# Ordering a decoder layer's instructions by a simulated timeline of all engines

## The chip, the cores and the metric

One core of one Trainium2 chip runs the whole program. The metric is device time in microseconds (us) of one execution, the median over several runs. Below, PE is the matmul engine, PEld its weight loads, DVE the vector engine, ACT the scalar engine, POOL the general engine (GpSimd) and SP the engine that issues most DMAs. A filler is a matmul that no step near it waits for.

## What is computed

One decoder layer over 1024 tokens of 1024 features, all in float32:

```python
x = LN(ALPHA * x + 0.5 * swiglu(x, ffn1))        # FFN1, 2816 hidden columns
z = x @ w_in                                     # 1024 x 3872
ret = retention(z[:, :2048])                     # 8 heads, chunks of 128 tokens
y   = rwkv7_scan(z[:, 2048:])                    # 8 heads of 64
    # per token: state = state*w - (state@kk) b^T + v k^T ;  y = state @ r
mixed = concat(silu(g) * groupnorm(ret), (groupnorm(y) + bonus) * gate)
x = LN(ALPHA * x + mixed @ w_out)
x = LN(ALPHA * x + 0.5 * swiglu(x, ffn2))        # FFN2
out = x + sigmoid(x @ w_gate + b) * (p @ w_proj) # PLE
```

## The kernel before

The three dense parts (FFN1, FFN2, PLE) run as blocked matmuls; float32 operands are split into a high and a low half, and `mm3` (L61 to L63) makes three matmuls of each pair. A part of FFN is written by `ffn_up` and `ffn_down`, which multiply seven products instead of eight per 2x2 block. Between FFN1 and FFN2 stands the `mixer`, in which this document is interested.

The mixer makes `z` in 28 column tiles (`z_tile`: two halves of 24 matmuls of 512 columns, weights from DMA and split by ACT and POOL); three more are made before it. A unit is a pair of RWKV heads over half of the tokens: eight units, named `u_h` for pair u and half h, in the order 0_0, 0_1, 1_0, ... 3_1. Each goes through these steps, all of small matmuls (64 to 256 columns) with DVE and ACT work between them:

1. `rw_inputs` and `rw_operands` read z, form the unit's operands, and write the strictly triangular matrices M (`m1pw`, copied at L1003);
2. `substitution` inverts the diagonal 32x32 blocks of eight such matrices: M goes out to DRAM and back as `iltw`, 31 pairs of tiny DVE operations follow (`itw` L1033 and `ixw` L1035, each needing the one before), the result goes out and comes back as `Xd`;
3. `doublings` builds the full inverse from it: a DVE transpose (`XTw`, L1047), then matmuls i1 to i5 with DVE operations between;
4. `rw_chunks` goes through four chunks of tokens one after the other; each needs the state `wst` that the one before left (L1095, L1131, L1135), makes `scpw` and `chw` on PE and masked copies `scz` (L1107, L1108) on DVE;
5. a group norm (`gstw`, `gnyw`, L797 to L805), four PE transposes `ytpw` (L812), the gate, and a DMA into `mixed`.

`retention` does the like for the retention heads (names ending in r; `yor`, `gnyr`, `ytpr`). `w_out_group` reads `mixed` back, splits it (`mw`), multiplies (`wopo`, 96 matmuls per group of two operands, 384 in all) and adds into `xacc` (L1192). Substitution of unit n+1 is written so that it can run beside the chunks of unit n.

The program states each step once. A scheduler decides where it stands on its engine: it keeps an engine's queue in the order of priorities, and code can push a step back by a number. The z tiles that unit 0_0 does not need and nearly all `wopo` are pushed back by 300:

```python
FILLER = -300
fill = {-1: ("w1", "t0"), 0: ("w2",), 1: ("t1",), 2: ("w3",), 3: ("t2",), 4: ("t3",)}
rows = {5: [((4, 0), (0, 1))], 6: [((5, 1), (0, 1))], 7: [((6, 2), (0, 1)), ((7, 3), (0,))]}
...
with self.tc.issue_after(self.gate):
    for f in fill.get(s, ()):
        with self.tc.high_priority(offset=FILLER):
            (rw if f[0] == "w" else rt)(int(f[1]))
```

`self.gate` is an instruction of the last `m1pw` (L1001). The fillers of unit s may not be placed ahead of it. After the last unit `normalise` begins layer norm LN2 and `w_out_group((7, 3), ..., (1,), True)` makes the last half group; FFN2's weights (`f2w`) are loaded from L101.

## Time and profile before

| what | value |
|---|---|
| median of 3 runs | 2365.26 us (2356.21 to 2366.05) |
| profiled execution | 2365.46 us, span of the trace 2363.3 us |
| PE busy | 96% of the span |
| PEld busy | 77% |
| DVE, ACT, POOL busy | 69%, 36%, 32% |
| mean granted TensorE clock | 0.977 of full speed |

The span is the time from the first to the last record. The 2.2 us around it belong to the execution and stand in every time. A busy share is an average over stages that have different limits, so the shares of single stages are needed as well.

### The profile page before, as it was taken

To read this page: it belongs to the slowest core of one execution; us is meant where nothing else is said; L and a number is where in the kernel's file an instruction comes from. 1 tells how busy PE (TensorE), PEld (TensorE's weight loads), DVE (VectorE), ACT (ScalarE), POOL (GpSimd) and SP (SyncE) were. 2 spreads that over 40 slices of the span, in tenths; PEclk is the share of its full clock that TensorE was granted. 3 is DMA by queue.
4 is the path that set the end of the run, shared out by engine and by line. 5 is a ranking of instruction groups with operands and counts; after the bars stand their busy time and mean duration, and the time that the engine had idled before them with its cause. 6 is when DMAs were issued, how large, how long until landed. Compare 5 with 4: busy or idle time off the path is not lost.

```text
span 2363.3 us, 30893 instructions
## 1 busy us (share of the span) xinstructions
PE 2262.3 (96%) x10753; PEld 1818.2 (77%) x10753; DVE 1622.9 (69%) x2702; ACT 842.7 (36%) x1430; POOL 751.9 (32%) x614
## 2 busy tenths in 40 slices
PE   6999999999999899999899999988999999999999
PEld 5788888788786677777677777766888788788787
DVE  7677777665782487773864876679676767866862
ACT  4323232344643433322322322264323232445550
POOL 3336454300102323332432423225555453000220
PEclk9999999999999999999999999999999999999999
DMA  4345555497336343323333353322465544974321
GB/s 144 112 155 181 182 179 165 149 337 239 90 133 199 116 124 99 108 79 93 113 92 112 98 175 120 98 89 85 156 196 161 188 159 139 350 257 155 112 76 41
DMA packets 288945, 345.97 MB, mean 146 GB/s; under 512 B 35571, under 2 KB 162134, under 8 KB 288790
## 3 DMA queue, kind: packets, MB, share of 16 engines
q1 hardware_dynamic: 284208, 331.37, 43.6%
q0 software_dynamic: 3328, 12.06, 1.3%
q8 instruction: 85, 1.39, 0.2%
q10 hardware_dynamic: 1254, 0.58, 0.1%
q14 instruction: 70, 0.57, 0.1%
HBM read 237.50 MB, written 106.43 MB: 146 GB/s over the span
## 4 chain that ended last, share of the span: by engine, by line
PE 79%; DVE 14%; issue 2%; ACT 2%; DMA 1%; POOL 1%; SPq 0%; DVEq 0%; ACTq 0%; POOLq 0%
PE f1m L61 6%; PE f1m L62 6%; PE f1m L63 6%; PE f2m L61 5%; PE f2m L63 5%; PE f2m L62 5%; PE z L63 3%; PE z L61 3%; PE z L62 3%; DVE ixw L1035 2%; DVE itw L1033 2%; PE f1qa L62 1%; PE f1qa L61 1%; PE scpw L1099 1%; PE f1qa L63 1%
## 5 line engine op out<-in xcount | busy, mean ns | idle before, releaser
L63 PE MATMUL z<-x1Th,lo_win 128*128 128x512 f32 x448 | 191.3, 427 | 5.3 <-DVE lo_win L48 2.9
L61 PE MATMUL z<-x1Th,hi_win 128*128 128x512 f32 x448 | 191.1, 427 | 0.8 <-ACT hi_win L47 0.8
L62 PE MATMUL z<-x1Tl,hi_win 128*128 128x512 f32 x448 | 187.9, 420 | 0.0
L48 POOL TENSOR_TENSOR lo_win<-raw_win,hi_win 128x512 fp32r<-128x512 f32 x54 | 74.7, 1384 | 160.3 <-ACT hi_win L47 140.3
L1033 DVE TENSOR_TENSOR itw<-iltw,ixw 32x31 f32<-32x31 f32 (+15 forms) x248 | 104.5, 421 | 29.8 <-DMA iltw<-scrw 14.3
L1035 DVE TENSOR_TENSOR ixw<-ixw,itw 32x31 f32<-32x31 f32 (+15 forms) x248 | 108.9, 439 | 4.0
L63 PEld LDWEIGHTS z<-x1Th,lo_win 128*128 128x128 f32 x448 | 87.2, 195 | 26.4 <-POOL lo_win L48 4.0
L61 PEld LDWEIGHTS z<-x1Th,hi_win 128*128 128x128 f32 x448 | 87.5, 195 | 24.2 <-issue 3.8
L62 PEld LDWEIGHTS z<-x1Tl,hi_win 128*128 128x128 f32 x448 | 87.5, 195 | 20.3 <-issue 2.9
L149 POOL TENSOR_TENSOR f2tb<-f2tb,f2tb 128x512 f32<-128x512 f32 x44 | 71.9, 1634 | 91.5 <-DMA f2tb<-in_ffn_w_down 83.6
L48 DVE TENSOR_TENSOR f1hl<-f1s,f1hh 128x512 fp32r<-128x512 f32 x63 | 45.5, 723 | 61.6 <-ACT f1hh L47 61.6
L149 POOL TENSOR_TENSOR f1tb<-f1tb,f1tb 128x512 f32<-128x512 f32 x44 | 66.5, 1511 | 42.2 <-DMA f1tb<-in_ffn_w_down 35.7
L48 DVE TENSOR_TENSOR f2hl<-f2s,f2hh 128x512 fp32r<-128x512 f32 x63 | 44.8, 711 | 44.9 <-ACT f2hh L47 44.9
L47 ACT CAST f1hh<-f1s 128x512 fp32r<-128x512 f32 x63 | 39.2, 622 | 92.1 <-PE f1qa L62 42.3
L47 ACT CAST f2hh<-f2s 128x512 fp32r<-128x512 f32 x63 | 39.2, 623 | 89.8 <-PE f2qa L62 36.1
L659 ACT COPY zs<-z 128x512 f32<-128x512 f32 x56 | 32.7, 583 | 97.2 <-PE z L63 84.9
L108 DVE TENSOR_TENSOR f2S<-f2w 128x512 f32<-128x512 f32 x22 | 17.5, 800 | 72.1 <-DMA f2w<-in_ffn_w_gu 67.3
L47 ACT CAST hi_win<-raw_win 128x512 fp32r<-128x512 f32 x56 | 34.6, 619 | 90.2 <-PE z L62 82.2
L48 POOL TENSOR_TENSOR f1A12l<-f1w,f1A12h 128x512 fp32r<-128x512 f32 x22 | 30.9, 1408 | 106.8 <-ACT f1A12h L47 106.8
L62 PE MATMUL f2qa<-f2vl,f2hh 128*128 128x512 f32 x164 | 63.9, 390 | 0.5 <-DVE f2vl L48 0.5
L62 PE MATMUL f1qa<-f1vl,f1hh 128*128 128x512 f32 x164 | 63.9, 389 | 0.0
L63 PE MATMUL f2qa<-f2vh,f2hl 128*128 128x512 f32 x164 | 63.8, 389 | 0.0
(785 smaller groups left out, 7197.9 us busy)
## 6 DMA issues: line engine op xcount, KB each, us to landing
f1w<-in_ffn_w_gu SPq DMA_DIRECT2D x44, 512.0 KB
f2w<-in_ffn_w_gu SPq DMA_DIRECT2D x44, 512.0 KB
f1s<-hd SPq DMA_DIRECT2D x63, 256.0 KB
f2s<-hd SPq DMA_DIRECT2D x63, 256.0 KB
zs<-zs SPq DMA_DIRECT2D x56, 256.0 KB
raw_win<-in_w_in SPq DMA_DIRECT2D x54, 256.0 KB
f1tb<-in_ffn_w_down SPq DMA_DIRECT2D x44, 256.0 KB
wt<-f1tb SPq DMA_DIRECT2D x44, 256.0 KB
```

Source lines behind the costliest of these rows:

```text
L47: self.last_split = self.nc.scalar.copy(hi, src).ins
L48: (eng or self.nc.vector).tensor_tensor(out=lo, in0=src, in1=hi, op=ALU.subtract)
L61: mm(ps, a[0], b[0], start=first, stop=False)
L62: mm(ps, a[0], b[1], start=False, stop=False)
L63: mm(ps, a[1], b[0], start=False, stop=last)
L108: sub = lambda o, a, b, op=ALU.subtract: V.tensor_tensor(out=o, in0=a, in1=b, op=op)
L149: nc.gpsimd.tensor_tensor(out=t, in0=a, in1=b, op=ALU.subtract)
L659: nc.scalar.copy(zs, ps)
L1033: nc.vector.tensor_tensor(out=t, in0=lt[:, j, j + 1:].unsqueeze(2).broadcast_to([B, n, c]), in1=x[:, j:j + 1, 0:c].broadcast_to([B, n, c]) ...
L1035: nc.vector.tensor_tensor(out=x[:, j + 1:, 0:c], in0=x[:, j + 1:, 0:c], in1=t, op=ALU.add)
L1099: nc.tensor.matmul(ps[e][:, 0:2 * P], kp[rr, cs], ar[rr, c].rearrange("p a t -> p (a t)"), start=True, stop=True)
```

## The change

```diff
@@ kernel()
-    with tile.TileContext(nc) as tc:
+    with tile.TileContext(nc, schedule_with_timeline_sim=True) as tc:
         hybrid_layer(tc, A)
```

The scheduler places the steps by a simulated timeline of all engines, where it used a plain estimate for each operation. Every instruction of the program stays, with its operands: 9615 on PE, 2704 on DVE, 1451 on ACT, 619 on POOL and 1177 on SP in either build. Only their order on each engine differs. The up products of FFN1 after the first block, the up products of FFN2 and nearly all of the down products keep their order on PE; the mixer is ordered anew. The number of fillers on PE in each stretch, counted in the two orders (a stretch begins with its unit's first i1):

| | ahead of 0_0 | 0_0 | 0_1 | 1_0 | 1_1 | 2_0 | 2_1 | 3_0 | 3_1 | behind |
|---|---|---|---|---|---|---|---|---|---|---|
| before | 432 | 59 | 157 | 104 | 220 | 111 | 225 | 63 | 63 | 294 |
| after | 398 | 226 | 192 | 144 | 192 | 192 | 96 | 192 | 48 | 48 |

**First place.** PE at the end of unit 1_0 (`chw1_03` is its last chunk, `ytpw1_0` waits for its group norm, `z640_..` are fillers, `i1w1_1..` begins the next unit). Before, 26 fillers stand between the last chunk and `ytpw1_0`, of which the first are:

```order
L1143 MATMUL chw1_03_9171<-saw1_03_9179,scz3_6355 128x64
L62 MATMUL z640_0_8662<-x1Tl5_3703,hi_win640_1_8658 128x512
L63 MATMUL z640_0_8662<-x1Th_3697,lo_win640_1_8659 128x512
L61 MATMUL z640_0_8662<-x1Th_3697,hi_win640_1_8658 128x512
L62 MATMUL z640_0_8662<-x1Tl6_3704,hi_win640_1_8658 128x512
...
L63 MATMUL z640_1_8690<-x1Th_3697,lo_win640_1_8659 128x512
L812 MATMUL ytpw1_0_9206<-ident_58,gnyw1_0_9196 128x128 x4
```

In the changed order, at the same place:

```order
L1142 MATMUL chw1_03_9171<-wvtw1_0_8155,scz3_6355 128x64
L1143 MATMUL chw1_03_9171<-saw1_03_9179,scz3_6355 128x64
L1113 MATMUL chw1_10_9837<-wst1_6361,arw1_1_8854 128x128
L812 MATMUL ytpw1_0_9206<-ident_58,gnyw1_0_9196 128x128 x4
L1056 MATMUL i1w1_10_9767<-Xd_6345,M11_6344 128x128 x4
L812 MATMUL ytpr1_0_9401<-ident_58,gnyr1_0_9386 128x128
L1000 MATMUL m1pw2_00_9619<-arw2_0_9614,bbw2_0_9616 128x128 x4
```

The fillers have moved away from this place: `ytpw` follows the last chunk with one matmul between them, and the next unit's i1 stands behind it. The ends of the other units read alike.

**Second place.** DVE at the group norm of unit 1_1 (`gstw1_1`, `gnyw1_1`), while the substitution of 2_0 (`itw2_0..`, `ixw2_0`) is under way in the order before:

```order
L797 TENSOR_REDUCE gstw1_1_9955<-yrw1_1_9824 128x8
L1033 TENSOR_TENSOR itw2_011_9674<-iltw2_0_9633,ixw2_0_9638 32x240
L798 TENSOR_SCALAR gstw1_1_9955<-gstw1_1_9955 128x8
L1035 TENSOR_TENSOR ixw2_0_9638<-ixw2_0_9638,itw2_011_9674 32x20x12
L799 TENSOR_TENSOR gnyw1_1_9956<-yrw1_1_9824,gstw1_1_9955 128x512
L1033 TENSOR_TENSOR itw2_012_9677<-iltw2_0_9633,ixw2_0_9638 32x247
L1035 TENSOR_TENSOR ixw2_0_9638<-ixw2_0_9638,itw2_012_9677 32x19x13
L968 TENSOR_SCALAR rnw2_1_10039<-rnw2_1_10039 128x8
```

In the changed order:

```order
L1047 STREAM_TRANSPOSE XTw2_0_10588<-Xd_6345 128x1024
L992 TENSOR_TENSOR arw2_1_10438<-kkw2_1_10050,ePw2_1_10020 128x4x128
L797 TENSOR_REDUCE gstw1_1_9955<-yrw1_1_9824 128x8
L797 TENSOR_REDUCE gstr1_1_10141<-yor1_1_10118 128x8
L754 SCALAR_TENSOR_TENSOR wrw3_0_10819<-wzrw3_0_10816,pcol_1830,smrw3_0_10820 128x512
L798 TENSOR_SCALAR gstw1_1_9955<-gstw1_1_9955 128x8
L798 TENSOR_SCALAR gstr1_1_10141<-gstr1_1_10141 128x8
L799 TENSOR_TENSOR gnyw1_1_9956<-yrw1_1_9824,gstw1_1_9955 128x512
```

The substitution has moved: all 62 operations for the next unit stand in the first chunk of a unit, and the other three chunks and the group norm are free of them. The group norms of both kinds of heads now alternate.

**Third place.** PE at the end of the last unit, 3_1 (`wopo5`, `wopo7_1` are the output products). Before:

```order
L872 MATMUL yor3_1_12908<-rst1_6358,zqr3_1_12857 128x128
L875 MATMUL yor3_1_12908<-vtr3_1_12879,rscr3_1_12893 128x64 x2
L63 MATMUL wopo5_0_0_1_12501<-mw_11826 128x512
L61 MATMUL wopo5_0_0_1_12501<-mw_11826 128x512
L62 MATMUL wopo5_0_0_1_12501<-mw_11826 128x512
L812 MATMUL ytpw3_1_12835<-ident_58,gnyw3_1_12825 128x128 x4
```

In the changed order:

```order
L1142 MATMUL chw3_13_12808<-wvtw3_1_12120,scz3_6355 128x64
L1143 MATMUL chw3_13_12808<-saw3_13_12816,scz3_6355 128x64
L812 MATMUL ytpw3_1_12835<-ident_58,gnyw3_1_12825 128x128 x4
L812 MATMUL ytpr3_1_12947<-ident_58,gnyr3_1_12932 128x128 x4
L61 MATMUL wopo7_1_0_0_13244<-mw_11826 128x512
L62 MATMUL wopo7_1_0_0_13244<-mw_11826 128x512
L61 MATMUL wopo7_1_1_0_13252<-mw_11826 128x512
```

Before, 294 fillers stand behind the last chunk of 3_1; in the changed order these are the 48 of `wopo7_1`, the last half group, which needs the group norm's result by way of `mixed`.

## Rows read from the trace of the kernel before

**Rows 1.** The page: busy time of the engines, and the chain that ended last.

```profile
PE 2262.3 (96%) x10753; PEld 1818.2 (77%) x10753; DVE 1622.9 (69%) x2702; ACT 842.7 (36%) x1430; POOL 751.9 (32%) x614
PE 79%; DVE 14%; issue 2%; ACT 2%; DMA 1%; POOL 1%; SPq 0%; DVEq 0%; ACTq 0%; POOLq 0%
```

**Rows 2.** Windows by stage: busy us and instructions per engine, granted clock, DMA.

```profile
core 0: us, PE busy (x) PEld busy (x) DVE busy (x) ACT busy (x) POOL busy (x), PEclk, DMA share, GB/s
300.00:400.00 100.00, 100.00 (x443) 82.81 (x442) 73.71 (x82) 28.37 (x44) 55.77 (x37) 1.00 0.53 171
718.00:870.00 152.00, 138.21 (x567) 99.25 (x567) 68.60 (x135) 57.69 (x93) 46.67 (x63) 0.97 0.47 144
1016.00:1198.00 182.00, 170.97 (x952) 133.43 (x951) 119.17 (x271) 54.53 (x106) 66.47 (x62) 0.95 0.32 97
1483.00:1560.00 77.00, 73.70 (x332) 57.32 (x331) 54.76 (x98) 24.41 (x37) 21.44 (x18) 0.98 0.30 97
1560.00:1660.00 100.00, 85.52 (x371) 67.30 (x370) 86.68 (x119) 54.75 (x91) 41.43 (x27) 0.91 0.32 101
```

**Rows 3.** The transposes that open the units' doublings: ns min/median/max, first and last start.

```profile
L1047 DVE STREAM_TRANSPOSE XTw<-Xd x8: 1226/1236/1245, 867.2 to 1436.2; 128x1024 f32<-128x1024 f32 x8
```

**Rows 4.** Windows of 10 us inside the mixer, same columns as Rows 2.

```profile
1140.00:1150.00 10.00, 6.04 (x31) 4.84 (x31) 9.97 (x16) 3.99 (x7) 8.08 (x7) 0.96 0.27 81
1160.00:1170.00 10.00, 8.68 (x40) 7.63 (x41) 8.68 (x21) 0.00 (x0) 2.67 (x3) 0.66 0.44 151
1290.00:1300.00 10.00, 10.00 (x53) 7.22 (x52) 1.40 (x5) 2.44 (x6) 0.89 (x2) 1.00 0.18 45
```

**Rows 5.** Groups by line, whole trace and two tiles: busy, mean; or ns min/median/max.

```profile
L1033 DVE TENSOR_TENSOR itw<-iltw,ixw 32x31 f32<-32x31 f32 (+15 forms) x248 | 104.5, 421 | 29.8 <-DMA iltw<-scrw 14.3
L1035 DVE TENSOR_TENSOR ixw<-ixw,itw 32x31 f32<-32x31 f32 (+15 forms) x248 | 108.9, 439 | 4.0
L992 DVE TENSOR_TENSOR arw<-kkw,ePw x8: 671/691/1773, 779.2 to 1334.5; 128x512 f32<-128x512 f32 x8
```

**Rows 6.** Timeline at the end of unit 2_0: start, us, engine, operation.

```profile
1236.21 0.27 ACT L1144 COPY yrw<-chw 128x128 f32<-128x128 f32 x1 [1.34 <-PE chw L1143]
1237.80 0.67 DVE L797 TENSOR_REDUCE gstw<-yrw 128x8 f32<-128x512 f32 x1
1242.64 0.68 DVE L805 TENSOR_TENSOR gnyw<-gnyw,gstw 128x512 f32<-128x512 f32 x1
1243.38 0.65 PE L812 MATMUL ytpw<-ident,gnyw 128*128 128x128 f32 x4
1243.79 0.48 PE L63 MATMUL z<-x1Th,lo_win 128*128 128x512 f32 x1
```

**Rows 7.** Timeline of DVE around the substitution of unit 3_1.

```profile
1363.51 0.74 DVE L1003 COPY_PREDICATED M<-mask,m1pw 128x512 f32<-128x512 uint8 x1 [0.95 <-PE m1pw L1000]
1371.37 0.18 DVE L1033 TENSOR_TENSOR itw<-iltw,ixw 32x31 f32<-32x31 f32 x1 [4.89 <-DMA iltw<-scrw]
1418.41 0.17 DVE L1035 TENSOR_TENSOR ixw<-ixw,itw 32x31 f32<-32x31 f32 x1
1436.24 1.24 DVE L1047 STREAM_TRANSPOSE XTw<-Xd 128x1024 f32<-128x1024 f32 x1
```

**Rows 8.** Timeline behind the last chunk of unit 3_1.

```profile
1481.20 0.27 ACT L1144 COPY yrw<-chw 128x128 f32<-128x128 f32 x1 [2.12 <-PE chw L1143]
1492.12 0.60 PE L812 MATMUL ytpw<-ident,gnyw 128*128 128x128 f32 x4
1496.63 0.32 SPq L1155 DMA_DIRECT2D mixed<-wow  x1
1528.53 0.33 SPq L1169 DMA_DIRECT2D wo<-mixed  x1
1528.91 30.52 SPq L101 DMA_DIRECT2D f2w<-in_ffn_w_gu  x4
```

## The prediction

> **What bounds the kernel now.** I read the page first. PE is busy 96% of the span and makes up 79% of the chain that ended last, with DVE second at 14% [rows 1]. Where PE waits, the reader must look by stage. The windows show two kinds of stage [rows 2]. In FFN1 (300 to 400 us) PE runs 443 matmuls in 100 us, one each 0.226 us, with its weight loads busy 82.81 of 100 and the clock at 1.00: nothing is to be had there by order. In the mixer the weight loads are busy 99.25 of 152 us (65%), then 133.43 of 182 (73%): PE has room. The mixer runs from about 718 to 1560 us, 842 us, and it is the only long stage whose order changes.
>
> What the mixer holds of PE work I price from these rows. A filler costs 0.226 us as in FFN1. Units 1_0 and 1_1 (1016 to 1198 us) hold 952 matmuls, of which 104 + 220 = 324 are fillers by the count in the order, 73 us. The other 628 are small: four transposes of 128 columns take 0.41 us until the next matmul starts [rows 6], 0.10 each, and with 0.01 to 0.02 more for changes between large and small I take 0.115, so 72 us, or 36 us for each unit. That is 145 of 182 us. The other 37 us, some 18 a unit, are waits and slow stretches. What they wait for the 10 us windows show [rows 4]: at 1140 DVE is busy 9.97 and PE 6.04, and shortly after the clock is at 0.66 of full speed, between its 1.2 and 2.4 GHz levels within the window; at 1290 DVE is busy 1.40 and PE 10.00. Work for the two engines comes in turns.
>
> **The change part by part.** No instruction is added or removed, so the sum is one of waits. I use three marks that the transposes of Xd give [rows 3]. The first unit's is at 867.2 us, the last unit's at 1436.2, so before it is 149 us from 718 to the first, 569 for seven units (81.3 each), and 124 from the last to 1560.
>
> *Ahead of the first unit.* 398 fillers for 432: 34 x 0.226 = 8 us less, so 141. The rest of this stretch waits for the inputs of unit 0_0 either way.
>
> *Units 0_0 to 2_0.* They now hold 226 + 192 + 144 + 192 + 192 = 946 fillers, before 651. PE work is 946 x 0.226 = 214 and five units at 35 (my 36, less what 0_0 has not), 175: together 389 us. To that I add per unit three waits.
>
> First, the group norm. The order now puts only one other matmul between a unit's last chunk and `ytpw`, and i1 of the next unit behind it, so PE stands for as long as the group norm takes. It took 1236.21 to 1243.38 = 7.2 us behind unit 2_0 [rows 6], with seven substitution operations and other work of DVE in between, and 1481.20 to 1492.12 = 10.9 behind 3_1 [rows 8]. The eight operations themselves make about 4.2 us, by their rows between those shown. Free of the substitution but paired with the retention's group norm, it should lie between; I take 7, with 4.2 and 10.9 as the bounds. Before, 26 fillers (5.9 us) covered it.
>
> Second, the clock. Stretches where PE waited are followed by a clock of 0.66 for 10 us [rows 4], which is 3.4 us of full-speed work. I take 2, bounds 0 and 3.4.
>
> Third, the first chunk. All 62 substitution operations of the next unit now stand in it. At their means they are 31 x (0.421 + 0.439) = 26.7 us [rows 5], and with the chunk's own 13 or so of DVE work and the 10 us of doublings ahead of it I make this part 49 us, for some 44 of PE work: 5 us of wait, bounds 0 and 10.
>
> That is 14 us a unit, 70 for five, and 389 + 70 = 459; I also walked each unit's order by hand and came to 462, which I keep. Bounds are 389 + 5 x 4.2 = 410 and 389 + 5 x 24.3 = 510.
>
> Operations of DVE with two inputs are long or short in this trace: one multiplication of 512 columns took from 671 to 1773 ns, with 691 the median [rows 5]. The Trainium skill (SBUF — State Buffer, the section SBUF: two separate sides) says that such a DVE operation and one of GpSimd lock a shared port in turn, and that the loser waits for the other's whole instruction. These rows agree. If the new order brought the substitution clear of POOL, the third wait would go, 25 us over five units; nothing in the order keeps POOL's splits of z from falling there, so I don't count it.
>
> *Units 2_1 and 3_0.* Here the fillers run short: 96 and 192, so PE work is 22 + 36 = 58 and 43 + 32 = 75. The DVE queue, summed from the rows' medians for the operations that the order places in each unit, is 68 and 73 us. Behind the substitution stands the transpose of Xd, which waits for two transfers: M to DRAM and back, 1364.25 to 1371.37 = 7.1 us, and the result, 1418.41 to 1436.24 = 17.8 us at most [rows 7]. In 2_1 and 3_0 that transpose is placed ahead of group norm and state operations on DVE's queue, so they wait with it and PE with them. Adding the 7 and 12 or so that I believe uncovered, 87 and 92 to 96 us; I take 87 + 96 = 183, bounds 150 and 200. So seven units are 462 + 183 = 645 us, 76 more than before.
>
> *From the last unit's transpose to the end.* Before this took 124 us, because 294 fillers (66 us) stood behind the chunks; they covered the path group norm, gate, `mixed` out and back, split. Now 48 stand there, so the path is bare: chunks 41 us (44 in the trace, with 63 fillers for now 48), group norm 11 [rows 8], `ytpw` to the write of `mixed` 1492.12 to 1496.63 = 4.5 [rows 8], out, back and split about 8, and 48 x 0.226 = 11. The sum is 75 us, 49 less; bounds 65 and 90.
>
> *Behind the mixer.* LN2's statistics of the first half now stand ahead of the last products, and FFN2's first load, at 1528.91 [rows 8], need not wait for the last read of `mixed`. The 14.5 us that PE idles between 1560 and 1660 [rows 2] can shrink: -5, bounds -10 and 0. The start (0 to 80 us) is reordered as well, but DMA and DVE rule it; 0, bounds of 4 either way.
>
> **The sum.** 141 - 149 = -8; 645 - 569 = +76; 75 - 124 = -49; -5. Together +14 us. The profiled execution took 2365.46, its span 2363.3 plus 2.2 around it, and stands 0.2 above the median of the runs. So 2365.5 + 14 = 2379.
>
> **The rivals.**
> *The order pays in the units (faster).* The mixer has two regimes, and DVE's stretches at 1140 us are broken up when group norm and substitution no longer alternate and the fillers are spread. With the group norm at 4.2, and neither the clock nor the first chunk costing, five units take 410 us for my 462; allow half of that, and 26 us less gives 2353; all of it 2327. It decides from 3 us less wait per unit on. For it speaks the 1140 row, against it that PE must now stand at each unit's end. The Trainium skill (Perfetto Trace Analysis, Optimization Strategy) names interleaving regimes whose most contended engine differs as a way to gain, which is what the timeline attempts; the row at 1290, with DVE idle and PE full, agrees that there was something to interleave.
>
> *The tail costs more (slower).* If the transposes of Xd wait their full 17.8 us in 2_1 and 3_0 and the mixed path takes 90, that is +17 and +15, some 2411. It has the rows of unit 3_1 for it; against it, there is more time between M and use than I can see in the order.
>
> *No change.* PE is 96% busy and its work is the same; if the scheduler only moves waits about, 2365. The Trainium skill (Perfetto Trace Analysis, Identifying the Most-Contended Engine) calls the matmul share a poor measure and prefers that of weight loads; the 65 to 73% in the mixer against 83% in FFN1 agree that there are waits to move in both directions, so this is a balance and no bound.
>
> **How the numbers follow.** A difference of 0.5%, 12 us, is about what a measurement can tell from none. My forecast case, 2368 to 2395, has 0.37; the faster rival, 2320 to 2353, 0.26; the balance, 2353 to 2368, 0.17; the costlier tail, 2395 to 2430, 0.20. Faster by over 12 us is then 0.26; within 12 us, 2353 to 2377, holds the balance and a third of the forecast case with its centre in it, 0.28; slower 0.46. For 8 in 10 the range leaves out the outer part of the first and of the last: 2338 to 2415.
>
> **What would show it.** Right if PE stands 4 to 11 us between a unit's last `chw` and `ytpw`, if the starts of the eight Xd transposes span about 645 us, and if some 75 us follow the last one. Wrong if the five early units take under 90 us each, if 2_1 and 3_0 are as fast as their PE work, or if the substitution slows or speeds in its new place. FFN must keep its time; if it doesn't, the cause lies outside this sum.

## The result, and the profile after

The changed kernel takes 2452.0 us, median of 4 runs (2447.5 to 2454.1). The kernel before, on the same chip, takes 2360.7 (2356.0 to 2366.1). The ratio is 1.038, interval [1.035, 1.042]: 91 us slower, where +14 was forecast. The profiled execution took 2447.5 with a span of 2445.3, which is 82.0 us above the span of before; the account below is of these 82.

The busy line of the page answers to [rows 1]:

```profile
PE 2276.6 (93%) x10753; PEld 1850.5 (76%) x10753; DVE 1596.4 (65%) x2702; ACT 839.3 (34%) x1430; POOL 739.1 (30%) x614
```

PE has the same matmuls and is busy 14 us longer, though no work was added, and its idle time grew from 101 to 169 us. So there are two things to look for: waits, and matmuls that run longer.

The groups of the two marks that divide the mixer: the transposes answer to [rows 3]; each unit's first matmul i1 is shown for after, then, in the second fence, for before (ns min/median/max, first and last start).

```profile
L1047 DVE STREAM_TRANSPOSE XTw<-Xd x8: 1234/1245/1246, 884.1 to 1529.6; 128x1024 f32<-128x1024 f32 x8
L1056 PE MATMUL i1w<-Xd,M x128: 272/420/422, 885.2 to 1549.4; 128*128 128x128 f32 x128
```

```profile
L1056 PE MATMUL i1w<-Xd,M x128: 270/275/377, 870.6 to 1439.1; 128*128 128x128 f32 x128
```

The median i1 went from 275 to 420 ns with the same shape: 80 of the 128 now run at the low clock, all 16 in four units and half of them in two. The transposes span 645.5 us, the forecast figure, but the last one runs 16 us ahead of the matmul that needs it (1546.03), where it ran 1 us ahead of it before, so the forecast's mark flatters the order and its agreement is luck. Marked by the first i1 of a unit, the 82 us are:

| stretch (profiled executions) | before | after | change | forecast |
|---|---|---|---|---|
| start to the first i1 | 870.6 | 885.2 | +14.6 | -8 |
| five units, to the i1 of 2_1 | 389.2 | 483.9 | +94.7 | +76 with the next row |
| 2_1 and 3_0, to the i1 of 3_1 | 177.4 | 177.0 | -0.4 | |
| to the last `wopo` | 126.6 | 90.1 | -36.5 | -49 |
| behind it | 799.5 | 809.2 | +9.7 | -5 |

By the forecast's own mark, the transposes, the parts are +16.9 to the first one, +76.5 to the last unit's, -21.0 from there to the last `wopo`, and +9.7, where it said -8, +76, -49 and -5.

PE's waits of the changed kernel (us in total, times, longest us):

```profile
PE ytpw L812 <- DVE gnyw L805: 47.3, 8, 8.4
PE wopo L61 <- ACT mw L47: 9.7, 1, 9.7
PE f1m L61 <- DVE f1U L179: 9.0, 2, 4.8
PE f2m L61 <- DVE f2U L179: 8.2, 2, 4.6
PE chw L1138 <- DVE wst L1135: 7.9, 7, 2.1
PE tp L80 <- DVE x3Tl L85: 7.7, 3, 3.6
PE tp L80 <- ACT f1acc L568: 7.5, 3, 4.7
```

None of these stood among the longest waits of before, where `ytpw` took 2.5 us at one unit end and the largest was:

```profile
PE rnpw L812 <- ACT rbw L971: 8.6, 3, 4.0
```

Windows of the changed kernel, columns as in [rows 2]:

```profile
210.00:220.00 10.00, 5.86 (x16) 4.37 (x15) 7.46 (x9) 0.74 (x2) 3.47 (x3) 0.66 0.37 135
300.00:400.00 100.00, 95.18 (x409) 78.24 (x408) 68.01 (x83) 27.10 (x43) 48.60 (x33) 0.97 0.57 177
705.00:748.00 43.00, 33.45 (x143) 25.94 (x142) 25.43 (x51) 18.00 (x26) 3.13 (x5) 0.84 0.19 67
1010.00:1034.00 24.00, 24.00 (x128) 19.20 (x128) 23.04 (x55) 7.51 (x14) 6.20 (x6) 1.00 0.24 77
1079.00:1108.00 29.00, 29.00 (x160) 23.57 (x159) 13.85 (x32) 9.25 (x17) 10.96 (x12) 0.75 0.37 114
1445.00:1452.00 7.00, 0.65 (x3) 0.46 (x4) 5.90 (x11) 2.31 (x5) 1.40 (x3) 0.50 0.32 102
1452.00:1481.00 29.00, 27.33 (x155) 23.14 (x154) 13.84 (x30) 7.84 (x12) 8.93 (x7) 0.71 0.32 99
1604.00:1630.00 26.00, 8.84 (x29) 6.17 (x30) 17.19 (x39) 14.36 (x20) 7.45 (x8) 0.61 0.61 204
```

The reader is to see three things. FFN1, which had 443 matmuls in 300 to 400 us, has 409. A unit's end (1445 to 1452) leaves PE 0.65 of 7 us while DVE does the group norm, and the 29 us behind it have a clock of 0.71 although PE is busy for 27.3 of them: 29 x 0.29 = 8.4 us of full-speed work. The first chunk (1010 to 1034) has PE busy all of 24 us beside 23 us of DVE work, 18 of them the substitution: there the order does what a timeline should. The substitution doesn't lie in this chunk alone: it starts at 1000.9, in the doublings, and ends at 1039.6.

PE at the end of unit 0_0, which answers to [rows 6]:

```profile
976.60 0.44 PE L1113 MATMUL chw<-wst,arw 128*128 128x128 f32 x2
982.98 1.12 PE L812 MATMUL ytpw<-ident,gnyw 128*128 128x128 f32 x4 [5.94 <-DVE gnyw L805]
983.89 1.91 PE L1056 MATMUL i1w<-Xd,M 128*128 128x128 f32 x8
```

The last chunk is followed by a bare wait of 5.94 us. Then `ytpw` takes 1.12 us, for 0.65 in [rows 6], and eight i1 take 1.91. The waits at the eight ends are 5.9, 6.4, 5.6, 6.1, 8.4, 6.4, 2.1 and 6.5 us.

The gap in FFN1, by the timeline of SP, DVE and PE:

```profile
206.25 0.38 SPq L101 DMA_DIRECT2D f1w<-in_ffn_w_gu  x1
212.54 1.47 DVE L108 TENSOR_TENSOR f1S<-f1w 128x512 f32<-128x512 f32 x1 [10.89 <-DMA f1w<-in_ffn_w_gu]
213.94 0.68 DVE L179 TENSOR_TENSOR f1U<-f1m,f1U 128x512 f32<-128x512 f32 x1
214.76 0.77 PE L61 MATMUL f1m<-f1T4h,f1A22h 128*128 128x512 f32 x1 [4.14 <-DVE f1U L179]
215.33 0.63 PE L62 MATMUL f1m<-f1T4l,f1A22h 128*128 128x512 f32 x1
```

DVE waits 10.89 us for a weight tile that SP asked for at 206.25, and the addition `f1U` is queued behind that wait. PE needs `f1U` and stops for 4.14 us; its next matmuls follow each other at 0.43 us instead of 0.23, and the granted clock of that window is 0.66, between the levels of 1.2 and 2.4 GHz. Such gaps occur at 210 and 332 us in FFN1, and at 1828 and 1949 in FFN2.

### The profile page after: what moved, and what is told of

Same layout as the page of the kernel before. It is cut to its first block, busy times and chain, and to the rows that moved or that the text cites. A ratio compares the mean times of both kernels' runs of the same rounds, so it can differ in the third digit from the quotient of the medians.

```text
span 2445.3 us, 30873 instructions
## 1 busy us (share of the span) xinstructions
PE 2276.6 (93%) x10753; PEld 1850.5 (76%) x10753; DVE 1596.4 (65%) x2702; ACT 839.3 (34%) x1430; POOL 739.1 (30%) x614
## 4 chain that ended last, share of the span: by engine, by line
PE 46%; DVE 11%; DMA 4%; issue 2%; ACT 2%; POOL 1%; SPq 0%; DVEq 0%; ACTq 0%; POOLq 0%
PE f2m L61 4%; PE f2m L62 4%; PE f2m L63 4%; PE z L63 3%; PE z L62 3%; PE z L61 3%; DVE itw L1033 2%; DVE ixw L1035 2%; PE f2qa L62 1%; PE f2qa L63 1%; PE f2qa L61 1%; PE pg L62 1%; PE pg L61 1%; PE pg L63 1%; PE f2qb L63 1%
## 5 line engine op out<-in xcount | busy, mean ns | idle before, releaser
L61 PE MATMUL z<-x1Th,hi_win 128*128 128x512 f32 x448 | 184.5, 412 | 0.0
L63 PE MATMUL z<-x1Th,lo_win 128*128 128x512 f32 x448 | 182.7, 411 | 1.1 <-DVE lo_win L48 1.1
L62 PE MATMUL z<-x1Tl,hi_win 128*128 128x512 f32 x448 | 182.3, 407 | 0.0
L149 POOL TENSOR_TENSOR f2tb<-f2tb,f2tb 128x512 f32<-128x512 f32 x44 | 66.5, 1510 | 104.9 <-DMA f2tb<-in_ffn_w_down 91.7
L108 DVE TENSOR_TENSOR f1S<-f1w 128x512 f32<-128x512 f32 x22 | 20.1, 919 | 99.2 <-DMA f1w<-in_ffn_w_gu 79.7
L61 PE MATMUL wopo<-mw 128*128 128x512 f32 x128 | 57.4, 449 | 13.1 <-ACT mw L47 9.7
L63 PE MATMUL f1qa<-f1vh,f1hl 128*128 128x512 f32 x164 | 63.9, 389 | 0.0
```

The source lines that it names most:

```text
L61: mm(ps, a[0], b[0], start=first, stop=False)
L62: mm(ps, a[0], b[1], start=False, stop=False)
L63: mm(ps, a[1], b[0], start=False, stop=last)
L108: sub = lambda o, a, b, op=ALU.subtract: V.tensor_tensor(out=o, in0=a, in1=b, op=op)
L149: nc.gpsimd.tensor_tensor(out=t, in0=a, in1=b, op=ALU.subtract)
```

## The experiments

Two kinds of kernel were run. In the pinned ones, the kernel before gets one helper that queues every instruction behind the one that a list names, so that any order can be given exactly, and single rows can be put elsewhere:

```diff
+def pin(tc, nc):
+    ins = {i.name: i for i in nc.cur_bb.bb.instructions}
...
+        for a, b in zip(names, names[1:]):
+            tc.add_manual_dep(ins[b], a, mybir.DependencyInfo(
+                mybir.DependencyClass.NoSync, mybir.DependencyReason.DATA), reason="pin")
...
         hybrid_layer(tc, A)
+        pin(tc, nc)
```

For these the edit is shown as rows that moved. The others are short edits of the changed kernel. Ratios are to the kernel before on the same chip, which had medians of 2358 to 2361 us.

**1 and 2. Eight DVE operations of FFN, put back in the changed order, and moved in the order before.** DVE's rows of the second kernel against before, one of four such places:

```diff
+L108 TENSOR_TENSOR f1S_5_1876<-f1w_16_1866 128x512
 L179 TENSOR_TENSOR f1U_1214<-f1m_1_3_1476,f1U_1214 128x512
+L108 TENSOR_TENSOR f1w_16_1866<-f1w_5_1864,f1w_16_1866 128x512
 L214 TENSOR_TENSOR f1G_1213<-f1G_1213,f1U_1214 128x2048
...
-L108 TENSOR_TENSOR f1S_5_1876<-f1w_16_1866 128x512
-L108 TENSOR_TENSOR f1w_16_1866<-f1w_5_1864,f1w_16_1866 128x512
```

> The changed order, with eight DVE operations put back where the order before has them: S1 and S3 (L108) of blocks 5 and 8, part 0, in FFN1 and in FFN2, behind the last additions of the block before the one under way. Theory (DVE waits for a weight load with the additions that free PE's results queued behind it): the four stops of PE in the FFN stages go, about 6 us each with the slow clock behind them, 23 us in all; 2452 becomes about 2429, a ratio to before of 1.029. Rival (the loads are late and PE would wait for them anyhow): no change, 2452, ratio 1.038.

> The order before, with only the same eight DVE operations moved to where the changed order has them. Theory: PE stops four times in the FFN stages, the time rises by about 23 us from 2361 to 2384, ratio 1.010. Rival (in the order before the loads come early enough, since SP is not behind): no change, 2361.

Put back, they gave 2449.6, ratio 1.038 [1.033, 1.042]: nothing. PE's longest waits between 90 and 480 us:

```profile
PE parps L617 <- DMA prow<-in_rw_mu: 4.8, 1, 4.8
PE f1m L61 <- DVE f1G L179: 4.7, 4, 1.9
```

The two waits for `f1U`, 9.0 us before this edit, went down to 1.5, and others took their place: at 240 us PE now waits for a transfer of parameter rows (`prow`) that ACT issues. Moved in the order before, the eight cost 10 us: 2369.5, 1.004 [1.002, 1.007], for the 23 expected. So a position on DVE alone is not the cause; the weights come later as well: SP issued the load shown above at 206.25 us, and its like at 199.48 before.

**3. Fillers put back into the group norm of four units of the changed order.** At the end of 0_0, PE's last chunk went ahead of 24 z matmuls, so that these stand between it and `ytpw`:

```diff
+L1142 MATMUL chw_03_7583<-wvtw_0_6773,scz_6355 128x64
+L1143 MATMUL chw_03_7583<-saw_03_7591,scz_6355 128x64
 L61 MATMUL z_1_8002<-x1Th,hi_win_0_7964 128x512
...
-L1142 MATMUL chw_03_7583<-wvtw_0_6773,scz_6355 128x64
-L1143 MATMUL chw_03_7583<-saw_03_7591,scz_6355 128x64
 L1113 MATMUL chw_10_8253<-wst_6361,arw_1_7266 128x128
 L812 MATMUL ytpw_0_7620<-ident,gnyw_0_7608 128x128 x4
```

> The changed order, with 24 fillers (half a z tile that stands in the last two chunks of the unit) moved between the last chunk and the group norm's transposes at the ends of units 0_0, 0_1, 1_0 and 1_1; the copy of their result and the splits of the next tile's weights go behind the group norm on ACT and POOL. Theory (PE idle during the bare group norm, and the clock it loses by that): each end gets back 5.4 us of idle time and some 3 us of slow clock, 34 us in all, 2452 to about 2418, ratio 1.024. Rival 1 (the wait only moves into the chunks that lose the fillers): 2452, ratio 1.038. Rival 2 (the clock does not follow from the idle time): 22 us, about 2430, ratio 1.029.

It gave 2428.1, ratio 1.029 [1.024, 1.034]: 24 us less than the changed kernel. PE's longest wait, and then the group of i1:

```profile
PE ytpw L812 <- DVE gnyw L805: 26.1, 7, 9.1
```

```profile
L1056 PE MATMUL i1w<-Xd,M x128: 270/275/423, 885.5 to 1531.4; 128*128 128x128 f32 x128
```

The wait fell by 21 us, and behind the four covered ends 4 of the 64 i1 run at the low clock, where 48 did. The time alone is that of the second rival, by which the clock doesn't follow from the wait. The trace speaks against it: over the 26 us behind these ends the clock is 1.00, 1.00, 0.93 and 1.00, where the changed kernel has 0.86, 0.75, 0.94 and 0.94 over 26 to 29 us, which is some 12 us of full-speed work. But PE stands idle for 9.5 of these 104 us, where it stood for 2 of 109, and the first chunks take some 6 us more. So wait and clock are both real, a part comes back as other waits, and what is left of a cover is 6 us a unit.

**4. The reverse: `ytpw` bare in the order before.** 97 fillers were moved behind `ytpw` at the ends of 1_0, 1_1, 2_0 and 2_1:

```diff
 L1143 MATMUL chw_03_9171<-saw_03_9179,scz_6355 128x64
+L812 MATMUL rnpw_0_9288<-ident,rbw_0_9286 128x128 x4
+L812 MATMUL ytpw_0_9206<-ident,gnyw_0_9196 128x128 x4
 L62 MATMUL z_0_8662<-x1Tl_3703,hi_win_1_8658 128x512
...
-L812 MATMUL ytpw_0_9206<-ident,gnyw_0_9196 128x128 x4
```

> The order before, with the 97 fillers that stand between the last chunk and the group norm's transposes of units 1_0, 1_1, 2_0 and 2_1 moved to right behind these transposes. Theory: 97 x 0.227 = 22 us of PE idle time appear at the four ends and 3 us of slow clock behind each, 34 us in all, 2361 to 2395, ratio 1.014. Rival (the moved fillers fill waits that PE has behind the transposes anyhow, where DVE is the busy engine): no change, 2361.

It gave 2374.6, ratio 1.007 [1.004, 1.010]: 15 us slower. PE's two longest waits:

```profile
PE rnpw L812 <- ACT rbw L971: 21.6, 4, 7.7
PE ytpw L812 <- DVE gnyw L805: 6.5, 2, 5.1
```

The first was 8.6 before, the second 2.5, so 17 of the 22 us appear as wait, and the time is about half of the 34 expected. What is missing above all is the clock: over the 20 us behind these four ends it is 0.93, 0.89, 0.87 and 0.89, where the order before has 0.91, 0.78, 0.91 and 0.74 with PE idle for 5 us of the 80; the moved fillers keep PE busy there for 79.4. So the price of a bare group norm depends on what stands behind it.

**5 and 6. FFN apart from the mixer.** The fifth has the changed order with all queues of both FFN stages as before; the sixth has the order before with these stages as changed.

> The changed order with the two FFN stages (the start to the middle of FFN1's down products, and FFN2 from its second block to the middle of its down products) put back into the order before on all five queues. Theory (the order of DVE and SP in the FFN stages costs by itself, and eight operations alone could not be put back because the queues around them had moved too): FFN1's 16 us and FFN2's 10 us go, 2452 becomes about 2426, ratio to before 1.028. Rival (the stops in FFN come with the runs, not with the order): no change, 2450, ratio 1.038.

> The order before with the same two FFN stages in the changed order on all five queues. Theory: 26 us more, 2360 to about 2386, ratio 1.011; at least the 10 us that eight of these operations cost alone. Rival (only those eight cost anything): 2370, ratio 1.004.

The fifth took 2419.3, ratio 1.024 [1.021, 1.027], 33 us less than the changed kernel; the sixth 2390.3, 1.012 [1.009, 1.016], 30 us more than before. The window of 300 to 400 us, first of the fifth, then of the sixth:

```profile
300.00:400.00 100.00, 100.00 (x443) 82.81 (x442) 73.79 (x87) 28.31 (x44) 51.91 (x36) 1.00 0.52 173
```

```profile
300.00:400.00 100.00, 95.98 (x413) 78.97 (x412) 68.71 (x86) 24.87 (x38) 44.37 (x30) 0.97 0.57 179
```

The gaps go and come with the queues of FFN, from both sides. Behind the first block, the up products of FFN1 take 380.7 us before, 395.8 changed, 380.7 in the fifth and 396.2 in the sixth. A third of the loss lies where the forecast put none. Both runs move all five queues of these stages together, the kernel's start included, so they don't tell SP's part from DVE's.

**7 to 9. The scheduler kept, with fillers gated.** The seventh holds the second half of five z tiles behind the unit's last chunk; the eighth does the same for the half group (7, 3) at the end of 3_1; the ninth also holds `z_first`, the z tiles at the end of FFN1, behind the last down product.

```diff
+LATE = (3328, 1664, 3456, 1792, 1920)
...
+            late = h == 1 and c0 in LATE
+            with self.tc.issue_after(self.last_ch) if late else nullcontext():
...
-                        with self.tc.high_priority(offset=FILLER):
+                        with self.tc.high_priority(offset=FILLER), self.tc.issue_after(self.last_ch) if ks == (7, 3) else nullcontext():
...
+                    with self.tc.issue_after(down):
```

> The changed kernel, still ordered by the timeline, where the second half of one z tile for each of the units 0_0 to 2_0 may only be placed behind that unit's last chunk; 24 fillers then stand ahead of the group norm's transposes at five unit ends. Theory (idle PE at a bare group norm): four ends gave 24 us when they were moved by hand, so five give 30, 2452 to about 2422, ratio 1.026. Rival (the scheduler opens the same wait elsewhere): 2452, ratio 1.038.

> As the kernel with five gated ends, and the 48 output products of the next to last half group may also only be placed behind the last chunk of unit 3_1. Theory (the last group norm and the way of mixed out and back are bare): 48 x 0.227 = 11 us of them are covered, 11 us below the kernel with five gated ends, about 2411, ratio 1.021. Rival (unit 3_1's chunks lose what the end gains, since there PE waits for the chain as well): equal to it, 2422.

> As the kernel with the gated tail, and z_first (the three z columns that are made at the end of FFN1) may only be placed behind the last down product, so that it lies beside layer norm LN1's second half. Theory (60 of its matmuls stood ahead of their place, and PE then waited 11 us for LN1 and ran slow): 12 us less, 2406 to about 2394, ratio to before 1.014. Rival (the down products then wait for what z_first covered): 2406, ratio 1.018.

They took 2411.7, 1.021 [1.018, 1.023]; 2405.8, 1.018 [1.016, 1.021]; and 2406.4, 1.019 [1.017, 1.022]. The five gates bring 40 us, 8 a unit, the largest single part. PE's longest waits of the seventh (its line numbers are 1 to 3 higher):

```profile
PE ytpw L815 <- DVE gnyw L808: 22.1, 6, 9.6
PE wopo L62 <- ACT mw L48: 10.5, 1, 10.5
```

The gate at 3_1 brings 6 more. The ninth brings nothing: `tp` no longer waits for `f1acc` but 8.4 us for `x1Tl`.

**10 to 12. Down to what is left.** The tenth is the ninth with FFN's queues as before. The eleventh also gates a `wopo` half behind 2_1. The twelfth is the eighth with FFN's queues and those of the end of FFN1 (600 to 735 us, layer norm and first z tiles) as before.

> The same with the two FFN stages in the order before on all five queues. Theory (the parts add up): 30 to 33 us less than with z_first held back, about 2362, ratio to before 1.001. Rival (the stages hide part of each other): 2375, ratio 1.006.

> The same, and the second half of the first output group (48 products) may only be placed behind the last chunk of unit 2_1, whose group norm is still bare (PE waits 9.7 us there). Theory: 8 to 10 us less than without it, about 2353, ratio to before 0.997. Rival (unit 3_0 then lacks the fillers that were moved ahead of it): 2362, ratio 1.001.

> As n2_gated_tail in the mixer, with both FFN stages and the end of FFN1 (layer norm LN1 and the first z tiles) in the order of before. Theory: the end of FFN1 is a loss of its own. n2's 2405.8 less the 23 us that the FFN order gave in p3, less 11 to 12 us for the stretch around 705 to 748 us, is 2371 (ratio about 1.004), and PE's waits for f1acc and x1Tl in that stretch go. Rival: that stretch is covered by the mixer's own start and a wait for z or x1T takes its place, so that the time stays at p3's 2383 (1.009).

They took 2383.2, 1.009 [1.007, 1.012]; 2381.3, 1.009 [1.007, 1.012]; and 2374.5, 1.006 [1.005, 1.008]. In the twelfth the first z tile starts at 721 us, 748 in the changed kernel, so the 43 us ahead of it answer to the window of 705 to 748 us above:

```profile
678.00:721.00 43.00, 43.00 (x203) 34.73 (x202) 28.52 (x54) 17.41 (x26) 4.99 (x7) 1.00 0.29 111
```

PE is busy all of these 43 us at a clock of 1.00, for 33.45 at 0.84, and its waits for `f1acc` and `x1Tl` are no longer among the longest. The end of FFN1 was worth 7 (by the ratios) to 9 us (by the medians) of the 11 expected. The tenth missed both of its values: 23 us came back, where the fifth gave 33. The eleventh covers the end of 2_1, whose wait of 9.7 us is gone, and yet its time is the tenth's. Unit 3_0 lost the 42 fillers that 2_1 gained, and its end keeps its wait of 4.9 us (4.7 in the tenth); `wopo` waits 8.3 us for `xacc`, 3.1 in the tenth. What it covered came back elsewhere; these waits are a part of that, and the rest isn't shown.

By medians, then, the 91 us are some 40 (group norms and their clock in five units), 6 (the last unit's), 23 to 33 (FFN), 8 (end of FFN1) and 16 left; the parts overlap a little, as FFN's prices of 33 alone and 23 behind the gates show. No version beat the kernel before.

## Why the prediction was wrong

The direction was right, and the main mechanism: PE stands bare at each unit's end. Of the signs that it named, the waits at the unit ends (5.6 to 8.4 us at seven of eight) and five early units of 90 to 104 us each came; the 75 us behind the last transpose were 107. The size was wrong by 77 us, and the time lay outside the range. By the prediction's steps:

*"FFN must keep its time; if it doesn't, the cause lies outside this sum"* is the step that failed. It put the start at 0 with bounds of 4 and took FFN's time as fixed, because the up and down products keep their order on PE. The fifth and sixth experiments price that at 33 and 30 us. It isn't the only miss: without these 33 the kernel takes 2419, still above the range's 2415, and the terms below make up the rest. PE's order was the wrong evidence: DVE, SP and POOL got another order, and one operation of DVE that waited 10.89 us for a transfer held the addition queued behind it, which PE needed. The 1.00 clock and 100.00 of 100 us in [rows 2] said that FFN had nothing to gain, and for that reason everything to lose.

*Ahead of the first unit, -8.* z's part did shrink, by 13 us. FFN1's up products and the step behind them took 17 longer, and the end of FFN1, which the sum doesn't have, 11: 60 matmuls of `z_first` now stand ahead of the last down products, where 3 did, so that layer norm has nothing beside it. The twelfth experiment shows 7 to 9 us for it; the ninth, which moved only `z_first`, shows that the other queues belong to it.

*Units 0_0 to 2_0, 462 us; measured 483.9.* The PE work is about right: priced at the median time of each shape it is 390, for 389 (an estimate; with the groups kept apart by line too it is some 410). What is over it is 94 us in place of 73; PE stands idle for 44 of them. The group norm measured 32.4 / 5 = 6.5 us of wait, for 7; with what the last chunks themselves lose around it, it comes to 9. The clock was mis-sized: 2 us a unit, bounds 0 and 3.4, from 10 us windows of a kernel in which PE hardly stood still [rows 4]. The stretches behind the five ends have clocks of 0.86, 0.75, 0.94, 0.94 and 0.75 over 26 to 29 us, which is 3.6 + 7.3 + 1.6 + 1.6 + 7.3 = 21 us, 4.3 a unit, beyond the upper bound in three of five. The first chunk was put at 5 us and lost 3, none of it as the wait that was forecast: PE is busy throughout. Small waits in chunks for `wst` and `saw`, 1.5 a unit, had no term. The substitution kept its pace in its new place (421 and 439 ns an operation before, 426 and 432 changed). Whether DVE and GpSimd hold each other up isn't decided by the row of 671 to 1773 ns: its two long operations, 1514 and 1773, ran beside GpSimd operations that had begun before them, but so did three that took 671 to 673.

The Trainium skill (TensorE: Matmul & The Clock Gate, HAM oscillation — how this bites in real kernels) describes a kernel that waits behind every group of matmuls and so starts every group cold, paying the change of clock each time. The median i1 of 420 ns agrees: that case is what this order makes of the units.

*2_1 and 3_0, 183 us; measured 177.* The size is right by luck, since the cause is another: PE stands idle for 18 us of it and the clock is 0.50 in 1445 to 1452 and 0.71 behind it, while DVE has no wait for a transfer among its longest between 1363 and 1530 us, so the 17.8 us of [rows 7] were covered.

*From the last unit to the end, -49; measured -36.5, by i1.* The path behind the chunks is as forecast: a wait of 6.5 us for the group norm, `mixed` written at 1615.02 and `mw` ready at 1622.84, which is the 9.7 us wait of `wopo`. What is too small is the chunks' 41 us, taken from a stretch in which PE was busy 44.97 of 45 us (1436.2 to 1481.2 before). Doublings and chunks now take 57 us, from 1546.0 to 1603.6, with the clock at 0.80 and 0.71 in 1546 to 1580.

*Behind the mixer, -5.* From the last `wopo` to FFN2's second block it did shrink, by 3. Then FFN2's up products took 8 longer, and its down products, with layer norm LN3 beside them, 6.

*The rival of no change* ("the scheduler only moves waits about") fails for a reason that the counts of fillers show. Units 0_0 to 3_0 hold 1234 fillers for 939, which is 295 x 0.226 = 67 us of PE work, and they became 94 us longer. Had the fillers filled waits, the units would have grown by less than 67. The tail lost 261 fillers, 59 us, and became only 36.5 shorter. The same work was taken from a place where it covered a path, and put where, taken together, it covered nothing.

*The faster rival* drew on interleaving. The first chunks show it, PE 24.00 and DVE 23.04 of 24 us. The price is that the fillers are spent there. The offset of 300 doesn't save them: it stands in both kernels, and the early units still hold 295 more. The likely reason, which no run tests, is that a simulated timeline gives an idle PE whatever is ready, and a filler nearly always is.

**What stays open.** The last 16 us. The trace of the twelfth run puts them in the mixer, whose units are still longer by more than its tail is shorter, and in layer norm LN3, where `tp` waits 7.7 us for `x3Tl`, 2.9 before. LN3's queues weren't put back by themselves. Two unit ends are also still bare in it, 9.6 us at 2_1 and 4.7 at 3_0:

```profile
PE ytpw L812 <- DVE gnyw L805: 16.7, 5, 9.6
```

The eleventh run shows that covering the first of them is not enough. Which queue of FFN carries its 30 us isn't separated. Why a clock stays low for 3 us behind one unit's end and for 15 behind another isn't settled either.

## What to carry to other kernels

A filler is worth what it covers where it stands. This scheduler put 295 more fillers into the early units and left the long waits bare; tie them to the instruction whose wait they are to cover (`issue_after`), which brought back 46 of 91 us here. When all queues are ordered anew, a stage that was at its bound can only lose: compare the order of every engine and of the DMA issues there, not only that of the busiest engine. Price a bare wait of PE with the slow matmuls behind it, from a place where PE really stood still.

## What was unexpected of the hardware

A wait of 4.14 us of PE in FFN1 was followed by about 5 us of matmuls at 0.43 us each, and waits of 5.6 to 8.4 us at unit ends by clocks of 0.71 to 0.94 over the next 26 to 29 us with PE busy nearly throughout. The same length of wait cost from 1.6 to 8.4 us of full-speed work. Behind the four bare ends of the fourth run, where large matmuls follow, the clock was no lower than in the order before. And an operation of DVE that waited 10.89 us for a transfer held PE for 4.14 us, though PE waited for the addition behind it and not for its result.
